# Feed-forward blocks 3, 5, 7 and 9 by eight products, block 10 by seven with a down product beside it, and all large buffers at one address remainder

## The chip, the core and the metric

The kernel runs on one core of one Trainium2 chip. The time is device microseconds (us) from launch to end. The median of 3 runs of the kernel before is 2426.34 us (2423.76 to 2428.74). The engines are named as in the profile: PE is TensorE's matmuls and PEld its weight loads, DVE is VectorE, ACT is ScalarE, POOL is GpSimd, and SP is SyncE, which here only issues DMAs.

## What is computed

Two layers over 256 rows of width 2048, float32. Layer 0 mixes with gated linear attention, layer 1 with an indexer and top-64 attention. After each mixer stands the same feed-forward step, and this is what the change touches:

```
def swiglu(h, w1, w3, w2):
    return (jax.nn.silu(h @ w1) * (h @ w3)) @ w2
...
    x = x + y
    x = x + swiglu(rmsnorm(x, norm_ffn[i]), ffn_w1[i], ffn_w3[i], ffn_w2[i])
return rmsnorm(x, norm_final)
```

`w1` and `w3` are 2048 x 5632, `w2` is 5632 x 2048. Each of them is read once from HBM per layer, in pieces of 512 x 512 (1 MB).

## The kernel before

**Precision.** TensorE multiplies in fp32r. Each operand is split in two: a high part (a cast) and a low part (what the cast left over). A product is then three matmuls: high by high, high by low, low by high. For a piece of weights ACT writes the high part `wh` (L135) and DVE the low part `wl` (L136); both come from `split_w`. The buffers `raw` (4), `wh` (3) and `wl` (3) are rings in the pool `wp`. Loads into `raw` stand in SP's queue in the order of use, so SP waits for the oldest of the four to be split.

**Feed-forward, up.** The 5632 columns are walked in 11 blocks of 512 (`b` from 0 to 10). For one block, h is seen as four parts: rows 0-127 and 128-255 by columns 0-1023 and 1024-2047. Sums and differences of these parts, the *forms* `A11`, `F7`, `A12`, `N22`, `F5`, `F3`, `F6`, lie ready in a pool called `fz` (tiles `fh...`, `fl...`). One product of a form with 1024 x 512 weights is 8 x 3 = 24 matmuls of 512 columns. There are two ways through a block:

- `plain` takes four products for each of w1 and w3, eight in all: 192 matmuls, 8 pieces loaded and split, no sums of weights.
- `pair` takes w1 and w3 together and needs seven products: 168 matmuls. It splits 14 pieces, since three of the seven products have sums of weights for an operand. These sums are made in place. DVE adds two (`plus`, L405), and DMAs that add in memory, issued by POOL, make two more (`plus_dma`, L408, two pieces each). The pieces that are summed live in four fixed homes: `v0`, `v1`, `v2` in `fz` and `g3` in the pool `res`. `turn` swaps which two hold `va` (summed by DMA) and which `vb` (summed by DVE). The products of a `pair` stand in the order A11, F5, F3, F6, F7, A12, N22; F6 waits for the first two adding DMAs, N22 for the other two.

**Feed-forward, down.** The block's result, tiles `u`, is transposed and split by `split_t` (in steps that `tick()` puts between the matmuls that follow) into a tile `g0`, `g1` or `g2`. `pieces` multiplies two such blocks with their 1024 rows of w2: 4 x 2 steps of 24 matmuls, with the sums added into `x`. A deque `down` holds these steps; `ffn` puts one step at each `yield` of `pair` or `plain`. A `pair` has eight yields, so it takes all eight steps. What is not done this way is returned by `ffn` and done afterwards by `residual`, which also starts the norm of the next stage or, at the end of the program, the final norm (`gemm_tail` for the last 512 columns).

**Which block goes which way (before).** `pair` is taken while `down` is not empty. A deque whose generator has given its last step but has not yet been asked again still counts as not empty. So blocks 0, 1 and 10 are plain, and blocks 2 to 9 are pairs. Blocks 2, 4, 6, 8 carry eight down steps each; blocks 3, 5, 7, 9 carry none. Blocks 8, 9 and 10 are left for `residual`: 4 x 3 x 24 = 288 matmuls per layer.

**Order on an engine.** Each engine works through its own list, in order; the lists come from a scheduler that places the instructions as they are written, with some moved ahead. A `pair`'s four home loads stand in SP's list among the `raw` loads.

**Addresses.** Pools follow each other in every partition of SBUF: `cst`, `res` (x, g), `wp` (raw, wh, wl), `cm` (u), `sm` (small), and then the pool of the stage (`gp`, `fz`, `dp`, at the end `fp`). In the built program, x, g, raw, wh, wl and u start at addresses with remainder 192 by 256. The stage's pool starts at remainder 128, and so do its tiles: the forms `fh`/`fl`, `v0` to `v2`, the operands `hh`/`hl` of the mixers' projections, and in `gemm_tail` the first `wh`/`wl` (taken from `fp`). In the pool `dp` some smaller tiles have other remainders.

Of the kernel before, what the change touches and what calls it, by code (L numbers as in the profile page):

```python
# [12 lines left out]
F32 = mybir.dt.float32  # L13
# [6 lines left out]
P = 128  # L20
# [3 lines left out]
NB = 512  # L24
# [31 lines left out]
def trunk(  # L56
# [9 lines left out]
    cst = ctx.enter_context(tc.tile_pool(name="cst", bufs=1))  # L66
# [3 lines left out]
    sm = ctx.enter_context(tc.tile_pool(name="sm", bufs=2))  # L70
# [13 lines left out]
            nc.sync.dma_start(x[t][n], x2[t, :, n * NB:(n + 1) * NB])  # L84


    neghalf = cst.tile([P, 8], F32, name="neghalf")
    nc.gpsimd.memset(neghalf, -0.5)
    warm = sm.tile([P, 8], F32, tag="warm", bufs=1, name="warm")
# [4 lines left out]
    cols = cst.tile([P, 72], F32, name="cols")  # L94


    sm.tile([P, 8], F32, tag="pad", bufs=1, name="pad")

    def gains(c0, srcs):

# [14 lines left out]
    def tick():  # L115

        while side:
            try:
                return next(side[0])
            except StopIteration:  # L120
                side.popleft()
# [9 lines left out]
    def split_w(raw, pool=wp):  # L131

        wh = pool.tile([P, 4, NB], F32R, tag="wh", bufs=3 if pool is wp else 1, name="wh")
        wl = pool.tile([P, 4, NB], F32R, tag="wl", bufs=3 if pool is wp else 1, name="wl")
        nc.scalar.copy(wh, raw)  # L135
        nc.vector.tensor_sub(wl, raw, wh.bitcast(F32))  # L136
        return wh, wl
# [70 lines left out]
    def split_t(src, hi, lo):  # L208

        for kk in range(2):  # L210
            tr = tr_p.tile([P, 2, SEQ], F32, tag="tr", name="tr")
            for t in range(NT):
                for k in range(2):
                    c = (2 * kk + k) * P
                    nc.tensor.transpose(tr[:, k, t * P:(t + 1) * P], src[t][:, c:c + P], ident)
            sl = slice(2 * kk, 2 * kk + 2)
            nc.scalar.copy(hi[:, sl, :], tr)
            nc.vector.tensor_sub(lo[:, sl, :], tr, hi[:, sl, :].bitcast(F32))
            yield
# [122 lines left out]
    def scaled(r, f, tag, w=NT):  # L342
        o = sm.tile([P, w], F32, tag=tag, name=tag)
        nc.gpsimd.tensor_scalar_mul(o, r, f)
        return o
# [13 lines left out]
    def hi_lo(i):  # L359
        g = res.tile([P, 2, 4, SEQ], F32R, tag=f"g{i}", name=f"g{i}")  # L360
        return g[:, 0], g[:, 1]

    def flush():
        while side:
            tick()
# [83 lines left out]
    def plain(nrm, ws, c0, done):  # L449

        for q, w in zip("12", ws):
            acc = [acc_p.tile([P, NB], F32, tag="acc", name="acc") for _ in range(3)]
            for g in range(4):
                raw = wp.tile([P, 4, NB], F32, tag="raw", bufs=RAW, name="raw")
                nc.sync.dma_start(raw, w[g * NB:(g + 1) * NB, c0:c0 + NB].rearrange("(k p) n -> p k n", p=P))
                wh, wl = split_w(raw)
                for bank, form, start, stop in ((0, "A11", True, True), (1, "F7", True, True)) if g < 2 else \
                        ((0, "A12", False, True), (2, "N22", True, True)):
                    hi, lo = nrm.forms[form]
                    for j in range(4):  # L460
                        k = 4 * (g % 2) + j
                        for i, (l_, r_) in enumerate(((hi, wh), (hi, wl), (lo, wh))):
                            nc.tensor.matmul(acc[bank], l_[:, k, :], r_[:, j, :], start=start and k == i == 0,  # L463
                                             stop=stop and k == 7 and i == 2, skip_group_check=not start)
                        if j % 2:
                            tick()
                if g == 1:
                    s1 = nrm.pool.tile([P, NB], F32, tag="s1", bufs=1, name="s1")
                    nc.scalar.copy(s1, acc[0])
                    nc.vector.tensor_add(s1, s1, acc[1])  # L470
                    yield
            nc.vector.tensor_sub(s1, s1, acc[2])
            done("1" + q, acc[0])
            done("2" + q, s1)
# [24 lines left out]
    def ffn(layer, nrm):  # L499

        w1, w3, w2 = ffn_w1[layer], ffn_w3[layer], ffn_w2[layer]
        sc = {}
        parts = []
        down = deque()
        for b in range(DFF // NB):
            us = [None] * NT

            def done(q, v):
                t = int(q[0]) - 1
                if q[1] == "1":  # L510
                    us[t] = cm.tile([P, NB], F32, tag="u", name="u")
                    nc.scalar.activation(us[t], v, AF.Tanh, scale=sc["h"][:, t:t + 1])
                    nc.vector.scalar_tensor_tensor(us[t], us[t], 1.0, v, op0=ALU.add, op1=ALU.mult)
                else:
                    nc.vector.scalar_tensor_tensor(us[t], us[t], sc["r2"][:, t:t + 1], v, op0=ALU.mult, op1=ALU.mult)

            for slot, _ in enumerate(pair(nrm, w1, w3, b * NB, b // 2 % 2, done) if down else plain(nrm, (w1, w3), b * NB, done)):
                if b == 0 and slot == 0:
                    flush()
                    r = nrm.rstd()  # L520
                    sc["h"] = scaled(r, 0.5, "rh")
                    sc["r2"] = sm.tile([P, NT], F32, tag="r2", name="r2")
                    nc.gpsimd.tensor_tensor(sc["r2"], r, sc["h"], op=ALU.mult)
                while down:
                    try:
                        next(down[0])
                        break
                    except StopIteration:
                        down.popleft()
            hi, lo = hi_lo(b % 3)  # L530
            side.append(split_t(us, hi, lo))
            parts.append((hi, lo, b * NB))
            if b % 2 and b < 8:
                down.append(pieces(w2, parts))
                parts = []
        while down:
            for _ in down.popleft():
                pass
        return w2, parts
# [480 lines left out]
    with tc.tile_pool(name="gp", bufs=2) as gp:  # L1020
        n0.begin(gp)
        down = gla(n0, gp)
        flush()
    with tc.tile_pool(name="fz0", bufs=1) as fz:
        n1.begin(fz)
        residual(gla_w_out[0], down, n1.update)
        down = ffn(0, n1)
        flush()
    with tc.tile_pool(name="dp", bufs=2) as dp:
# [3 lines left out]
        down = dsa(n2, dp)  # L1033
        flush()
    with tc.tile_pool(name="fz1", bufs=1) as fz:
        n3.begin(fz)
        residual(dsa_w_out[0], down, n3.update)
        down = ffn(1, n3)
        flush()
# [56 lines left out]
```

## Time and profile before

| | |
|---|---|
| median of 3 runs | 2426.34 us |
| profiled execution | 2430.86 us |
| its span, first to last instruction | 2429.1 us |
| mean granted TensorE clock | 0.973 |
| PE busy | 2281.5 us (94%) |
| DVE busy | 1645.9 us (68%) |
| ACT busy | 1183.5 us (49%) |
| HBM read | 489.59 MB |

The profile is of one execution. Matmuls are pipelined, so that one lasts about 390 ns while the next begins some 227 ns after it; the busy time of PE is the union. Where a stage is dense, the distance from one matmul's start to the next is the number to read. A window table gives, for a stretch of the span, its length, the busy time of each engine with the number of its instructions (x), the granted TensorE clock, and the share and rate of the DMA engines.

### The profile page before, as it was taken

How to read it: one execution, taken by the hardware profiler on the slowest of the kernel's cores; microseconds unless marked ns; L12 is line 12 of the kernel's file. 1: busy time of each engine (PE TensorE's matmuls, PEld its weight loads, DVE VectorE, ACT ScalarE, POOL GpSimd, SP SyncE). 2: the span in 40 equal slices, each digit the busy share in tenths (PEclk: the TensorE clock that was granted, in tenths of full speed). 3: DMA queues.
4: the chain of work that ended last, by engine and by line, in shares of the span. 5: the costliest groups of instructions: out<-in, count | busy, mean ns of one | idle time of the engine just before them, and what ended most of it. 6: DMA issues, size and time to landing. Idle time of an engine off the chain costs nothing.

```text
span 2429.1 us, 25156 instructions
## 1 busy us (share of the span) xinstructions
PE 2281.5 (94%) x10199; PEld 1857.5 (76%) x10199; DVE 1645.9 (68%) x1348; ACT 1183.5 (49%) x1053; POOL 112.8 (5%) x159
## 2 busy tenths in 40 slices
PE   9999999998897979989999999999988979889798
PEld 7888888876675867768888888888876867768687
DVE  6555456677886878865556655565786778878754
ACT  5545455454454445544444454454444545545443
POOL 0000000000000000000100000000000000000000
PEclk9999999999999989999999999999998999989899
DMA  8555466586877968775554545566677977779663
GB/s 280 164 174 180 148 219 232 172 233 194 232 242 207 286 184 222 229 205 187 182 173 139 191 157 174 174 219 212 176 235 201 293 182 225 230 190 311 138 218 112
DMA packets 254773, 493.36 MB, mean 203 GB/s; under 512 B 8200, under 2 KB 20832, under 8 KB 254528
## 3 DMA queue, kind: packets, MB, share of 16 engines
q1 hardware_dynamic: 219856, 423.33, 51.1%
q0 software_dynamic: 33792, 67.11, 16.0%
q8 instruction: 80, 1.31, 0.2%
q10 hardware_dynamic: 1008, 1.31, 0.2%
q14 instruction: 37, 0.30, 0.0%
HBM read 489.59 MB, written 2.12 MB: 202 GB/s over the span
## 4 chain that ended last, share of the span: by engine, by line
PE 59%; issue 21%; DMA 9%; DVE 8%; ACT 2%; POOL 1%; SPq 0%; POOLq 0%; ACTq 0%; DVEq 0%
PE acc L201 11%; PE acc L203 11%; PE acc L202 11%; PE acc L463 10%; DMA g<-in_ffn_w 6%; PE acc L393 6%; DVE wl L136 5%; DMA v<-in_ffn_w 3%; PE down L490 2%; ACT wh L135 2%; PE down L491 2%; PE down L489 2%; DVE v L405 1%; POOL v L408 1%; PE trq L827 0%
## 5 line engine op out<-in xcount | busy, mean ns | idle before, releaser
L192 DVE TENSOR_TENSOR wl<-raw,wh 128x2048 fp32r<-128x2048 f32 (+3 forms) x161 | 350.1, 2176 | 314.8 <-ACT wh L191 314.6
L136 DVE TENSOR_TENSOR wl<-raw,wh 128x2048 fp32r<-128x2048 f32 x179 | 409.5, 2289 | 184.7 <-ACT wh L135 184.7
L135 ACT CAST wh<-raw 128x2048 fp32r<-128x2048 f32 x179 | 342.3, 1912 | 392.6 <-PE down L491 144.3
L191 ACT CAST wh<-raw 128x2048 fp32r<-128x2048 f32 (+3 forms) x161 | 291.9, 1815 | 278.8 <-PE acc L203 217.7
L136 DVE TENSOR_TENSOR wl<-v,wh 128x2048 fp32r<-128x2048 f32 x120 | 272.7, 2286 | 83.1 <-ACT wh L135 83.1
L201 PE MATMUL acc<-wh,hh 128*128 128x512 f32 (+3 forms) x832 | 327.1, 393 | 0.0
L135 ACT CAST wh<-v 128x2048 fp32r<-128x2048 f32 x120 | 227.4, 1904 | 198.9 <-DMA v<-in_ffn_w 99.9
L203 PE MATMUL acc<-wh,hl 128*128 128x512 f32 (+3 forms) x832 | 318.4, 383 | 0.0
L202 PE MATMUL acc<-wl,hh 128*128 128x512 f32 (+3 forms) x832 | 317.0, 381 | 0.5 <-DVE wl L192 0.5
L393 PE MATMUL acc<-wh,fhF 128*128 128x512 f32 x512 | 216.5, 426 | 59.3 <-ACT wh L135 59.2
L393 PE MATMUL acc<-wl,fhF 128*128 128x512 f32 x512 | 216.0, 422 | 30.9 <-DVE wl L136 30.9
L490 PE MATMUL down<-wl,g 128*128 128x512 f32 x512 | 204.0, 398 | 9.3 <-DVE wl L136 9.3
L393 PE MATMUL acc<-wh,flF 128*128 128x512 f32 x512 | 212.2, 414 | 0.0
L491 PE MATMUL down<-wh,g 128*128 128x512 f32 x512 | 202.9, 396 | 0.0
L489 PE MATMUL down<-wh,g 128*128 128x512 f32 x512 | 200.3, 394 | 0.0
L203 PEld LDWEIGHTS acc<-wh,hl 128*128 128x128 f32 x832 | 156.2, 188 | 30.8
L202 PEld LDWEIGHTS acc<-wl,hh 128*128 128x128 f32 x832 | 156.6, 188 | 30.3 <-issue 1.7
L201 PEld LDWEIGHTS acc<-wh,hh 128*128 128x128 f32 x832 | 156.5, 188 | 28.9 <-issue 1.9
L393 PEld LDWEIGHTS acc<-wh,fhF 128*128 128x128 f32 x512 | 103.9, 205 | 91.2 <-ACT wh L135 68.3
L201 PE MATMUL acc<-wh,g 128*128 128x512 f32 x424 | 167.2, 394 | 0.0
L203 PE MATMUL acc<-wh,g 128*128 128x512 f32 x424 | 165.5, 390 | 0.0
L202 PE MATMUL acc<-wl,g 128*128 128x512 f32 x424 | 165.4, 390 | 0.0
(282 smaller groups left out, 3608.6 us busy)
## 6 DMA issues: line engine op xcount, KB each, us to landing
raw<-in_ffn_w SPq DMA_DIRECT2D x200, 1024.0 KB, 5.8
v<-in_ffn_w SPq DMA_DIRECT2D x48, 1024.0 KB, 6.6
v<-in_ffn_w POOLq DMA_DIRECT2D x48, 1024.0 KB, 9.4
raw<-in_dsa_w_in SPq DMA_DIRECT2D x48, 1024.0 KB, 5.1
raw<-in_gla_w_in SPq DMA_DIRECT2D x40, 1024.0 KB, 5.1
raw<-in_gla_w_out SPq DMA_DIRECT2D x16, 1024.0 KB, 5.2
g<-in_ffn_w SPq DMA_DIRECT2D x16, 1024.0 KB, 6.7
g<-in_ffn_w POOLq DMA_DIRECT2D x16, 1024.0 KB, 13.3
```

Of the source, the lines that this page charges most:

```text
L135: nc.scalar.copy(wh, raw)
L136: nc.vector.tensor_sub(wl, raw, wh.bitcast(F32))
L191: a = nc.scalar.copy(wh[:, sl, :n], raw[:, sl, :n])
L192: v = nc.vector.tensor_sub(wl[:, sl, :n], raw[:, sl, :n], wh[:, sl, :n].bitcast(F32))
L201: nc.tensor.matmul(acc[t][:, :n], hi[:, k, ts_], wh[:, k, :n], start=start, stop=False)
L202: nc.tensor.matmul(acc[t][:, :n], hi[:, k, ts_], wl[:, k, :n], start=False, stop=False)
L203: nc.tensor.matmul(acc[t][:, :n], lo[:, k, ts_], wh[:, k, :n], start=False, stop=last)
L393: nc.tensor.matmul(acc, l_[:, k, :], r_[:, j, :], start=start and k == i == 0, stop=stop and k == 7 and i == 2, skip_group_check=not start)
L463: nc.tensor.matmul(acc[bank], l_[:, k, :], r_[:, j, :], start=start and k == i == 0, stop=stop and k == 7 and i == 2, skip_group_check=not ...
L489: nc.tensor.matmul(acc[t], hi[:, k, ts_], wh[:, k, :], start=start, stop=False)
L490: nc.tensor.matmul(acc[t], hi[:, k, ts_], wl[:, k, :], start=False, stop=False)
L491: nc.tensor.matmul(acc[t], lo[:, k, ts_], wh[:, k, :], start=False, stop=last)
```

## The change

Three things. (1) The way through a block is now chosen by its number: blocks 2, 4, 6, 8 and 10 are pairs, the others plain. (2) The down steps of blocks 8 and 9 are put in the deque too, so block 10 carries them; `residual` is left with block 10 alone, 96 matmuls. (3) A tile of 64 bytes is put ahead in `cst`, and a dummy in `sm` grows from 32 to 96 bytes. In the built program x, g, raw, wh, wl, u, and the stage's forms, homes and `hh`/`hl` then all start at remainder 0 by 256.

```
+    cst.tile([P, 16], F32, name="pad")
     neghalf = cst.tile([P, 8], F32, name="neghalf")
...
-    sm.tile([P, 8], F32, tag="pad", bufs=1, name="pad")
+    sm.tile([P, 24], F32, tag="pad", bufs=1, name="pad")
...
-            for slot, _ in enumerate(pair(nrm, w1, w3, b * NB, b // 2 % 2, done) if down else plain(nrm, (w1, w3), b * NB, done)):
+            for slot, _ in enumerate(pair(nrm, w1, w3, b * NB, b // 2 % 2, done) if b in range(2, 11, 2) else plain(nrm, (w1, w3), b * NB, done)):
...
-            if b % 2 and b < 8:
+            if b % 2:
                 down.append(pieces(w2, parts))
                 parts = []
```

Per layer this is four pairs fewer, one pair more, and the same w2 work in other places. Lines of the changed kernel are one higher than those of the one before.

First place: SP's list in layer 0, from the last loads of block 2 on. Before, block 3 is a pair. `v_4058`, `v_4060` are its homes v0, v1, and `v_4054`, `g_4056` its v2, g3; L380 with `raw` is a piece of weights that is multiplied once, L482 a piece of w2.

```order
L482 DMA raw<-in_ffn_w 128x4x512
L380 DMA v_4058<-in_ffn_w 128x4x512
L380 DMA v_4060<-in_ffn_w 128x4x512
L482 DMA raw<-in_ffn_w 128x4x512 x2
L380 DMA raw<-in_ffn_w 128x4x512 x2
L380 DMA v_4054<-in_ffn_w 128x4x512
L380 DMA g_4056<-in_ffn_w 128x4x512
L380 DMA raw<-in_ffn_w 128x4x512 x2
L482 DMA raw<-in_ffn_w 128x4x512 x2
```

Now block 3 is plain (its pieces are L456), and the home loads between are those of block 4: `v_4332`, `v_4334` are v0, v1, and `v_4336`, `g_4338` are v2, g3.

```order
L483 DMA raw<-in_ffn_w 128x4x512
L381 DMA v_4332<-in_ffn_w 128x4x512
L381 DMA v_4334<-in_ffn_w 128x4x512
L483 DMA raw<-in_ffn_w 128x4x512 x2
L456 DMA raw<-in_ffn_w 128x4x512 x2
L381 DMA v_4336<-in_ffn_w 128x4x512
L381 DMA g_4338<-in_ffn_w 128x4x512
L456 DMA raw<-in_ffn_w 128x4x512 x6
L483 DMA raw<-in_ffn_w 128x4x512 x2
```

The home loads stand at the same places of the list, but what they load is used a whole block later.

Second place: DVE's list in layer 0, inside block 3. Before, a stretch of the pair of block 3; each `wl` is one split of 2.29 us in the trace, L405 a sum of two pieces, and y, w, s sums of products.

```order
L136 TENSOR_TENSOR wl<-raw,wh 128x2048
L405 TENSOR_TENSOR v_4060<-v_4060,raw 128x2048
L423 TENSOR_TENSOR y<-acc,s_4111 128x512
L136 TENSOR_TENSOR wl<-raw,wh 128x2048
L136 TENSOR_TENSOR wl<-v_4054,wh 128x2048
L136 TENSOR_TENSOR wl<-g_4056,wh 128x2048
L136 TENSOR_TENSOR wl<-v_4058,wh 128x2048
L136 TENSOR_TENSOR wl<-v_4060,wh 128x2048
L431 TENSOR_TENSOR w<-acc,s_4111 128x512
```

Now, the middle of the plain block 3, up to the first split of block 4 (`v_4332`):

```order
L219 TENSOR_TENSOR g_4054<-tr,g_4054 128x512 x2
L137 TENSOR_TENSOR wl<-raw,wh 128x2048
L471 TENSOR_TENSOR s_4132<-s_4132,acc 128x512
L137 TENSOR_TENSOR wl<-raw,wh 128x2048 x2
L514 SCALAR_TENSOR_TENSOR u<-u,acc 128x512
L473 TENSOR_TENSOR s_4132<-s_4132,acc 128x512
L137 TENSOR_TENSOR wl<-raw,wh 128x2048
L514 SCALAR_TENSOR_TENSOR u<-u,s_4132 128x512
L137 TENSOR_TENSOR wl<-raw,wh 128x2048
L471 TENSOR_TENSOR s_4265<-s_4265,acc 128x512
L137 TENSOR_TENSOR wl<-v_4332,wh 128x2048
```

No split of block 3 reads a home any longer, so none of them stands behind an adding DMA.

Third place: SP's list at the end of layer 0. Before, block 10 is plain (L455), and `residual` loads twelve pieces of w2 (L185) ahead of the next mixer's weights:

```order
L380 DMA raw<-in_ffn_w 128x4x512 x2
L455 DMA raw<-in_ffn_w 128x4x512 x8
L185 DMA raw<-in_ffn_w 128x4x512 x6
L758 DMA rb<-in_rel_bias 32x16
L185 DMA raw<-in_ffn_w 128x4x512 x6
L185 DMA raw<-in_dsa_w_in 128x4x400 x4
```

Now block 10 is a pair with eight down steps (L483), and `residual` loads four pieces:

```order
L483 DMA raw<-in_ffn_w 128x4x512 x3
L381 DMA raw<-in_ffn_w 128x4x512 x2
L483 DMA raw<-in_ffn_w 128x4x512 x3
L186 DMA raw<-in_ffn_w 128x4x512 x4
L186 DMA raw<-in_dsa_w_in 128x4x400
L759 DMA rb<-in_rel_bias 32x16
L186 DMA raw<-in_dsa_w_in 128x4x400 x3
```

Eight pieces of w2 have moved from `residual` into block 10.

## The prediction

> **What bounds the kernel now.** I read a table of windows first, one window for each feed-forward block, cut at the first matmul of each block. Columns: start:end and length, then busy us (and instructions) of PE, PEld, DVE, ACT and POOL, then the granted clock, the DMA share and GB/s. Ten rows are blocks 2 to 10 and `residual` of layer 0; the seven below are layer 1: block 2, blocks 3+4, 5+6, 7+8, block 9, block 10, and `residual` to the end of the span.
>
> ```profile
> 485.92:571.08 85.16, 83.33 (x370) 68.23 (x369) 69.50 (x46) 44.62 (x27) 5.41 (x4) 1.00 0.85 247
> 571.08:630.64 59.56, 44.48 (x177) 34.10 (x176) 40.28 (x26) 28.29 (x18) 5.17 (x4) 0.91 0.77 200
> 630.64:718.20 87.56, 84.01 (x369) 68.22 (x368) 76.45 (x50) 45.53 (x28) 5.19 (x4) 1.00 0.83 248
> 718.20:777.60 59.40, 44.69 (x177) 34.15 (x176) 40.28 (x26) 28.30 (x18) 5.19 (x4) 0.91 0.77 200
> 777.60:866.09 88.49, 84.34 (x370) 68.12 (x368) 76.39 (x50) 45.33 (x28) 5.19 (x4) 1.00 0.83 246
> 866.09:926.05 59.96, 45.63 (x177) 35.28 (x176) 40.36 (x26) 28.29 (x18) 5.19 (x4) 0.89 0.77 198
> 926.05:1015.12 89.07, 85.49 (x369) 69.32 (x368) 76.74 (x50) 45.51 (x28) 5.19 (x4) 0.98 0.83 244
> 1015.12:1072.00 56.88, 44.62 (x178) 34.49 (x177) 41.56 (x27) 28.54 (x18) 5.19 (x4) 0.91 0.65 148
> 1072.00:1117.24 45.24, 45.24 (x206) 37.11 (x204) 27.29 (x21) 19.63 (x16) 0.00 (x0) 1.00 0.61 210
> 1117.24:1186.05 68.81, 68.81 (x320) 56.68 (x318) 38.47 (x35) 31.54 (x38) 0.68 (x4) 1.00 0.54 174
> 1718.60:1802.95 84.35, 83.19 (x369) 68.22 (x368) 69.48 (x46) 44.63 (x27) 5.23 (x4) 1.00 0.85 249
> 1802.95:1952.56 149.61, 133.02 (x545) 106.20 (x544) 116.93 (x75) 73.83 (x46) 10.37 (x8) 0.93 0.80 225
> 1952.56:2102.41 149.85, 132.89 (x545) 106.31 (x544) 116.91 (x75) 73.85 (x46) 10.37 (x8) 0.93 0.79 224
> 2102.41:2250.95 148.54, 132.24 (x545) 105.59 (x544) 117.11 (x75) 74.03 (x46) 10.37 (x8) 0.92 0.81 227
> 2250.95:2309.38 58.43, 45.91 (x177) 35.61 (x176) 41.52 (x27) 28.53 (x18) 5.18 (x4) 0.88 0.63 144
> 2309.38:2354.60 45.22, 45.22 (x205) 37.11 (x204) 27.46 (x21) 19.62 (x16) 0.00 (x0) 1.00 0.61 210
> 2354.60:2429.08 74.48, 66.24 (x295) 54.30 (x293) 37.35 (x36) 28.20 (x32) 1.11 (x2) 0.98 0.41 141
> ```
>
> Three kinds of block are to be seen. A pair with down steps (blocks 2, 4, 6, 8) is nearly all PE: 83 to 85 us busy. Block 10, plain, is all PE: 45.24 of 45.24. A pair alone (3, 5, 7, 9), a *quiet* pair, has the fewest matmuls and still takes 56.9 to 60 us, of which PE is busy for some 45: 12 to 15 us are holes, at a clock of 0.88 to 0.91 instead of 1.00. So eight products take less time there than seven. What holds the seven is in POOL's timeline of block 3 (start, length, what, and in brackets the idle time before and who ended it):
>
> ```profile
> 580.42 1.28 POOL L408 DMA_DIRECT2D v<-in_ffn_w  x1 [49.62 <-issue]
> 590.18 1.30 POOL L408 DMA_DIRECT2D g<-in_ffn_w  x1 [8.47 <-DMA v<-in_ffn_w]
> 601.07 1.29 POOL L408 DMA_DIRECT2D v<-in_ffn_w  x1 [9.60 <-DMA g<-in_ffn_w]
> 609.99 1.30 POOL L408 DMA_DIRECT2D g<-in_ffn_w  x1 [7.63 <-DVE wl L136]
> ```
>
> The four adding DMAs start about 10 us apart, and twice one waits for the one before to land. The first two lie between the splits of F5 and of F6, the last two between those of F6 and of N22. Four in a row need about 40 us. In 85 us of a pair with down steps that is covered; among the 168 matmuls of a quiet pair it is not.
>
> **The way of the blocks.** Durations come from the profiled execution of 2430.86 us (span 2429.1); the sum is made against that and carried over to the median of 2426.34, which is 4.5 lower.
>
> *Quiet pairs become plain.* Layer 0: 59.56 + 59.40 + 59.96 + 56.88 = 235.80 us now. A plain block is 45.24 (row of block 10, which also follows a pair and already pays the transposes of the block ahead of it), so four are 180.96: **-54.84**. The 24 matmuls more that each takes are in the 45.24. The splits fall from 14 to 8 a block, and neither POOL nor a home is waited for. Late next would be DVE at 27.29 or the DMA share of 0.61: neither is near.
>
> *Pairs 4, 6, 8 follow a plain block.* They take 87.56 + 88.49 + 89.07 = 265.12 us now. Block 2 is the one pair that already follows a plain block: 85.16. The rest of the work is the same, but after a quiet pair the homes are loaded late, since N22 of that pair still reads them; in the new list the loads stand a block ahead, as they did for block 2. 3 x 85.16 = 255.48: **-9.64**. I keep the hold of 1.8 us (85.16 less 83.33 busy) that remains in block 2, where F6 waits for the second adding DMA.
>
> *Block 10 and `residual`.* Now 45.24 + 68.81 = 114.05. Then block 10 is a pair with down steps, 85.16, and `residual` loses 192 of its 288 matmuls at 0.2268 us (worked out below), 43.55, so it is 25.26. What covered is gone in one place: the first product of `residual` was that of block 8, long ready, and is now block 10's own, which has to be transposed, cast and split first. The 48 down matmuls at the end of block 10 cover the making of `u`, not the split. No row shows this wait. From below it is 0 (in the row of `residual` PE has no idle time: 68.81 of 68.81), from above the 1.8 us of block 2's hold; I take 1. Together 111.42: **-2.63**. Eight norm steps now go with 96 matmuls instead of 288. That is still ahead of DVE: of its 38.47 us, eight splits of 2.29 go, which leaves 20 beside PE's 25.
>
> Layer 0 in all: -67.11.
>
> *Layer 1.* Blocks 3 to 8: 149.61 + 149.85 + 148.54 = 448.00, then 3 x (45.22 + 84.35) = 388.71: **-59.29**. Block 9: 58.43 to 45.22, **-13.21**. Block 10 with the end: 45.22 + 74.48 = 119.70, then 84.35 + 74.48 - 43.55 + 1.5 = 116.78, **-2.92**. The 1.5 are 0.5 for the split and 1 for the tail: the closing work of rows 0-127 (sum, norm, scaling, DVE and ACT in order) was hidden behind 36 matmuls and now has 12, 2.7 us, and what stands behind it on DVE and ACT is the closing work of rows 128-255, which ends the kernel. The bounds are 0 and 5.5 (the tail of 74.48 - 66.24 = 8.2, less the 2.7); I stay near 0, since only the DVE and ACT steps queue and not the chain. Layer 1 in all: -75.42.
>
> Sum of (1) and (2): **-142.5 us**.
>
> **The remainders.** Next the starts of matmuls in dense stretches (start, length, engine, line, what). First the last gemm: the first 12 matmuls of each half have `wh`, `wl` in `fp` (remainder 128) against `g` (192); from the 19th to the 25th both are at 192.
>
> ```profile
> 2404.16 0.39 PE L152 MATMUL acc<-wh,g 128*128 128x512 f32 x1
> ...
> 2406.96 0.39 PE L152 MATMUL acc<-wh,g 128*128 128x512 f32 x1
> ...
> 2408.34 0.39 PE L152 MATMUL acc<-wh,g 128*128 128x512 f32 x1
> ...
> 2409.70 0.39 PE L152 MATMUL acc<-wh,g 128*128 128x512 f32 x1
> ```
>
> 12 matmuls in 2.80 us are 233.3 ns each; 6 in 1.36 us are 226.7. Line, shapes and `g` are the same; the home of `wh`, `wl` is not. Next 24 matmuls of a pair, `wh` at 192 and the form at 128, and behind them 24 down matmuls, both at 192:
>
> ```profile
> 532.84 0.39 PE L393 MATMUL acc<-wh,fhF 128*128 128x512 f32 x1
> ...
> 538.33 0.39 PE L489 MATMUL down<-wh,g 128*128 128x512 f32 x1
> ...
> 543.77 0.39 PE L393 MATMUL acc<-wh,fhA 128*128 128x512 f32 x1
> ```
>
> 5.49 / 24 = 228.8 ns, and 5.44 / 24 = 226.8 (0.2268 above). So unequal remainders cost 2 to 6.6 ns a matmul. After the change they are equal, at 0. The matmuls that gain: forms, 6 x 192 + 5 x 168 = 1992 a layer, 3984 in all; and those on `hh`/`hl`, 3 x 736 by the rows of the groups, of which this is one:
>
> ```profile
> L203 PE MATMUL acc<-wh,hl 128*128 128x512 f32 x736 | 289.4, 393 | 0.0
> ```
>
> 3984 + 2208 = 6192 at 2.1 ns (between the 2.0 above and somewhat more, as I count no others): **-13.0 us**. All of it is on the path, as PE bounds every stage that is left. Equal remainders at 0 are not in the trace, only at 192. The bounds: no gain (0), or, if 0 is as bad as the worst row, 6192 x (233.3 - 228.8) and some 2900 matmuls on `g` x (233.3 - 226.8): +47 us. I take the row with equal remainders, the nearest. DVE and ACT I cost at nothing: a split of `v` (128 into 192) takes what one of `raw` (192 into 192) takes, 2286 and 2289 ns by these groups:
>
> ```profile
> L136 DVE TENSOR_TENSOR wl<-raw,wh 128x2048 fp32r<-128x2048 f32 x179 | 409.5, 2289 | 184.7 <-ACT wh L135 184.7
> ...
> L136 DVE TENSOR_TENSOR wl<-v,wh 128x2048 fp32r<-128x2048 f32 x120 | 272.7, 2286 | 83.1 <-ACT wh L135 83.1
> ```
>
> [...] The rows above differ by 6.6 ns with nothing changed but a buffer's place, so I follow the rows.
>
> **Sum.** 142.5 + 13.0 = 155.5 us less: 2430.86 becomes 2275.3, and from the median, 2426.34 - 155.5 = 2270.8. Forecast **2271 us**.
>
> **Rivals.**
> - *The remainders do nothing* (the change does not do what its third part says). For it: the rows with equal remainders are at other lines or parts of a gemm than most of those that should gain. Against: the last gemm. Time: 2271 + 13 = 2284. Chance 0.12.
> - *Pairs 4 to 8 keep their hold.* If the 2.4 to 3.9 us over block 2 come not from the homes but from the adding DMAs meeting more loads, they stay. 9.64 come back in layer 0, and in layer 1 between that and 19.7 (448.00 less three quiet pairs at 58.43 and three pairs at 84.35); I take 12: 2293. Against it: DMA share and rate in block 2 are as high (0.85, 247) as in the later ones. Chance 0.10.
> - *Late pieces after a pair* (the slower end). SP is in order, and in the first place of the list the home loads v2, g3 stand ahead of six pieces of the plain block and wait for N22's split. If SP were held there until four pieces, the whole ring, were used up, PE would lose four groups of 24 matmuls, 21.8 us, at the four joints of pair to plain in each layer: 2271 + 174 = 2445. It decides from 19.4 us a joint. Against it: N22 is split ahead of its matmuls, 72 or more matmuls (N22 and the down steps) follow that need only pieces loaded already, and DMA has room. A loss of a few us at a joint is likelier. Chance 0.02 for the full loss, 0.06 for one of 1 to 3 us a joint (2279 to 2295).
> - *Remainder 0 is worse than 192*: up to 2284 + 47 = 2331. Chance 0.03.
> - *More is won*: the hold of F6 goes too, 1.8 and 1.2 us in ten pairs: 2256. Chance 0.05.
>
> The forecast itself, 2261 to 2281, has the remaining 0.62. Range **2256 to 2293**: it takes in the remainders at nothing and the pairs that keep their hold, and leaves out the late pieces, the bad remainder and a little on each side. A measurement here can tell about 0.2%, 5 us. Faster by more than that: 0.97, as every case but the full loss lies below 2421; within: 0.01; slower: 0.02.
>
> **What would show it.** In windows cut in the same way: plain blocks 3 to 9 at 44 to 46 us with PE busy throughout and the clock at 1.00; pairs 4 to 10 at 84 to 86; `residual` of layer 0 at 24 to 28; 40 adding DMAs instead of 64 and still about 10 us apart. Dense matmuls on forms and `hh` 227 ns apart instead of 229: if they stay at 229, the third part has no effect. A plain block with holes at its start would show the late pieces; a pair of 88 us the hold that stays. The forecast is wrong if PE is idle for more than some 30 us in the feed-forward stages, or if the rest of the kernel, which the change leaves alone but for addresses, moves by more than its part of the 13 us.

## The result, and the profile after

| | us | ratio to before, 95% interval |
|---|---|---|
| kernel before, 4 runs on the same chip | 2427.06 (2423.76 to 2428.74) | |
| changed kernel, 4 runs | **2293.0** (2285.74 to 2298.71) | 0.9448 [0.9418, 0.9477] |
| forecast | 2271, range 2256 to 2293 | |

The change takes off 134 us where the forecast had 155: the sign and the bulk are right, and 22 us are missing, at the very end of the range. The profiled execution took 2298.71 us (span 2296.9), the longest of the four; against it the sum of the prediction, 2275.3, is **23.4 short**. The HBM read falls from 489.59 to 464.43 MB: `w1` and `w3` are not read just once, since the adding DMAs of a pair read four of its pieces a second time, and 24 such pieces of 1 MB are saved.

First the table of windows of the changed kernel, cut at the first matmul of each block as before: blocks 2, 3, 4, 6, 8, 10 and `residual` of layer 0, then of layer 1 blocks 2, 3, 4, 6, 8, block 10 with the wait behind it, and the end. (Blocks 5, 7, 9 read like block 3.) Columns: start:end and length, busy us (and instructions) of PE, PEld, DVE, ACT and POOL, granted clock, DMA share, GB/s.

```profile
483.98:568.63 84.65, 82.97 (x370) 68.11 (x368) 67.32 (x45) 44.70 (x27) 5.42 (x4) 1.00 0.87 261
568.63:613.09 44.46, 44.46 (x202) 36.83 (x200) 27.77 (x20) 18.86 (x14) 0.00 (x0) 1.00 0.52 165
613.09:697.69 84.60, 82.94 (x370) 68.11 (x368) 67.29 (x45) 44.69 (x27) 5.17 (x4) 1.00 0.88 261
...
742.15:829.24 87.09, 84.83 (x369) 69.26 (x368) 67.57 (x45) 44.69 (x27) 5.19 (x4) 0.98 0.87 253
...
873.70:957.79 84.09, 82.95 (x369) 68.13 (x368) 67.30 (x45) 44.70 (x27) 5.19 (x4) 1.00 0.88 263
...
1002.25:1089.31 87.06, 84.64 (x369) 69.12 (x368) 67.48 (x45) 44.68 (x27) 5.87 (x8) 0.98 0.75 205
1089.31:1117.50 28.19, 26.26 (x130) 21.21 (x129) 19.50 (x26) 16.08 (x29) 0.00 (x0) 1.00 0.47 150
1647.66:1734.16 86.50, 84.68 (x369) 69.25 (x368) 67.59 (x45) 44.67 (x27) 5.23 (x4) 0.98 0.87 255
1734.16:1778.62 44.46, 44.46 (x201) 36.82 (x200) 27.76 (x20) 18.86 (x14) 0.00 (x0) 1.00 0.50 165
1778.62:1866.05 87.43, 84.87 (x370) 69.26 (x368) 67.56 (x45) 44.68 (x27) 5.18 (x4) 0.98 0.86 253
...
1910.51:1999.11 88.60, 86.09 (x369) 70.17 (x368) 67.64 (x45) 44.67 (x27) 5.19 (x4) 0.96 0.86 249
...
2043.57:2130.09 86.52, 84.70 (x370) 69.25 (x368) 67.59 (x45) 44.70 (x27) 5.19 (x4) 0.98 0.88 255
...
2174.55:2264.51 89.96, 85.91 (x378) 70.00 (x376) 70.66 (x48) 48.93 (x31) 5.19 (x4) 0.98 0.71 199
2264.51:2296.90 32.39, 22.39 (x96) 17.86 (x96) 15.64 (x25) 8.90 (x21) 1.11 (x2) 0.90 0.17 66
```

The plain blocks are what was forecast, and better: 44.46 us, all of it PE. What is off is the pairs. Three of layer 0 lie at 84.1 to 84.7; the other two and all of layer 1 at 86.5 and more, with 1.8 to 2.6 us without a matmul (4.05 in the last, whose window takes in the wait behind it) and a clock of 0.96 to 0.98. Something inside a pair takes 2 to 4 us more than I had kept for it.

Where it is, the groups of PE show at once (line, shapes, count | busy us, mean ns | idle before them and who ended it). These are the form F's matmuls in pairs:

```profile
L394 PE MATMUL acc<-wl,fhF 128*128 128x512 f32 x320 | 130.2, 407 | 17.3 <-DVE wl L137 17.3
...
L394 PE MATMUL acc<-wh,fhF 128*128 128x512 f32 x320 | 128.9, 403 | 3.1 <-ACT wh L136 3.1
```

Together 20.4 us of idle PE stand in front of a split. The forms F5, F3, F6 and F7 share this row. PE's timeline of block 6, layer 0, says which it is: the second half of F6 (start, length, what, idle before it):

```profile
775.84 0.39 PE L394 MATMUL acc<-wh,fhF 128*128 128x512 f32 x1
...
779.16 0.50 PE L394 MATMUL acc<-wh,fhF 128*128 128x512 f32 x1 [0.44 <-ACT wh L136]
781.49 0.50 PE L394 MATMUL acc<-wl,fhF 128*128 128x512 f32 x1 [1.82 <-DVE wl L137]
...
782.95 0.63 PE L394 MATMUL acc<-wh,flF 128*128 128x512 f32 x1
783.38 0.63 PE L394 MATMUL acc<-wh,fhF 128*128 128x512 f32 x1
...
785.71 0.40 PE L490 MATMUL down<-wh,g 128*128 128x512 f32 x1
```

F6 should take 24 x 0.2268 = 5.44 us and takes 785.71 - 775.84 = 9.87. There are two losses in it. PE waits 0.44 us for the high part and 1.82 for the low part of the second piece. Then its matmuls come 0.43 us apart instead of 0.227 (782.95, 783.38): the granted clock is 0.50 from 781.99 to 785.40, for 3.4 us, which costs another 1.7. What the split waited for stands in ACT's and POOL's timelines of the same block:

```profile
777.20 1.91 ACT L136 CAST wh<-g 128x2048 fp32r<-128x2048 f32 x1 [7.41 <-DMA g<-in_ffn_w]
```

```profile
752.92 1.29 POOL L409 DMA_DIRECT2D v<-in_ffn_w  x1 [95.08 <-issue]
762.04 1.30 POOL L409 DMA_DIRECT2D g<-in_ffn_w  x1 [7.82 <-DVE y L424]
777.42 1.29 POOL L409 DMA_DIRECT2D v<-in_ffn_w  x1 [14.08 <-DMA g<-in_ffn_w]
```

ACT stood idle for 7.41 us until the second adding DMA had landed. That DMA was issued at 762.04 and landed at 777.1, 35.0 us after the block's first matmul at 742.15; then the cast takes 1.91 and the low part 2.29 before PE can go on. Measured from the first matmul of F6 to that of the down step behind it, in all ten pairs, F6 takes 7.44, 7.40, 9.87, 6.88, 9.85 us in layer 0 and 9.28, 9.60, 10.75, 9.28, 9.41 in layer 1: 89.8 instead of 54.4, so **35.4 us** are lost there. 20.4 of them are the idle time of the two rows above. About 11 are half clock: eight stretches of 3.41 us, less the holes in them, lose half of their length, 13 us, of which 1.9 fall on the down steps behind F6. The rest comes with the longer matmuls at the edges of the holes (some 0.3 us in each F6 that saw no half clock).

### The profile page after: what moved, and what is told of

It is laid out like the page before. It is cut to its first block, busy times and chain, and to the rows that moved or that the text cites. A ratio compares the mean times of both kernels' runs of the same rounds, so it can differ in the third digit from the quotient of the medians.

```text
span 2296.9 us, 25246 instructions
## 1 busy us (share of the span) xinstructions
PE 2256.8 (98%) x10343; PEld 1862.9 (81%) x10343; DVE 1526.7 (66%) x1298; ACT 1122.6 (49%) x1023; POOL 81.6 (4%) x135
## 3 DMA queue, kind: packets, MB, share of 16 engines
q0 software_dynamic: 21120, 41.95, 10.6%
HBM read 464.43 MB, written 2.12 MB: 203 GB/s over the span
## 4 chain that ended last, share of the span: by engine, by line
PE 57%; issue 30%; DMA 7%; DVE 3%; ACT 2%; POOL 1%; SPq 0%; POOLq 0%; ACTq 0%
PE acc L204 11%; PE acc L202 10%; PE acc L203 10%; PE acc L464 10%; PE acc L394 5%; DMA g<-in_ffn_w 4%; DMA v<-in_ffn_w 2%; PE down L490 2%; PE down L491 2%; PE down L492 2%; DVE wl L137 2%; ACT wh L136 1%; POOL v L409 1%; DVE wl L193 0%; PE tr L216 0%
## 5 line engine op out<-in xcount | busy, mean ns | idle before, releaser
L137 DVE TENSOR_TENSOR wl<-raw,wh 128x2048 fp32r<-128x2048 f32 x217 | 496.8, 2290 | 242.9 <-ACT wh L136 241.8
L492 PE MATMUL down<-wh,g 128*128 128x512 f32 x640 | 249.6, 390 | 0.0
L490 PE MATMUL down<-wh,g 128*128 128x512 f32 x640 | 248.3, 391 | 0.0
L137 DVE TENSOR_TENSOR wl<-v,wh 128x2048 fp32r<-128x2048 f32 x72 | 164.4, 2287 | 51.4 <-ACT wh L136 51.4
L136 ACT CAST wh<-v 128x2048 fp32r<-128x2048 f32 x72 | 137.6, 1911 | 107.2 <-PE acc L394 44.7
L464 PE MATMUL acc<-wh,fhA 128*128 128x512 f32 x384 | 150.7, 393 | 0.2
L464 PE MATMUL acc<-wh,flA 128*128 128x512 f32 x384 | 149.6, 390 | 0.0
L464 PE MATMUL acc<-wl,fhA 128*128 128x512 f32 x384 | 149.6, 390 | 0.0
L394 PE MATMUL acc<-wl,fhF 128*128 128x512 f32 x320 | 130.2, 407 | 17.3 <-DVE wl L137 17.3
L491 PEld LDWEIGHTS down<-wl,g 128*128 128x128 f32 x640 | 120.6, 188 | 26.3
L490 PEld LDWEIGHTS down<-wh,g 128*128 128x128 f32 x640 | 121.0, 189 | 25.3
L492 PEld LDWEIGHTS down<-wh,g 128*128 128x128 f32 x640 | 120.6, 188 | 24.9
```

The costliest lines, as they stand in the source:

```text
L394: nc.tensor.matmul(acc, l_[:, k, :], r_[:, j, :], start=start and k == i == 0, stop=stop and k == 7 and i == 2, skip_group_check=not start)
L490: nc.tensor.matmul(acc[t], hi[:, k, ts_], wh[:, k, :], start=start, stop=False)
L491: nc.tensor.matmul(acc[t], hi[:, k, ts_], wl[:, k, :], start=False, stop=False)
L492: nc.tensor.matmul(acc[t], lo[:, k, ts_], wh[:, k, :], start=False, stop=last)
```

## The experiments

Lines named are those of the changed kernel. Each kernel was run beside the kernel before, which gave 2427.7, 2429.1 and 2426.8 us on the three chips.

**The two halves of the change apart.** `e1_order_alone` is the changed kernel at the old addresses, `e2_places_alone` the old order at the new ones:

```
 e1 (against the changed kernel)                    e2 (against the kernel before)
-    cst.tile([P, 16], F32, name="pad")             +    cst.tile([P, 16], F32, name="pad")
...
-    sm.tile([P, 24], F32, tag="pad", ...)          -    sm.tile([P, 8], F32, tag="pad", ...)
+    sm.tile([P, 8], F32, tag="pad", ...)           +    sm.tile([P, 24], F32, tag="pad", ...)
```

> The new choice of blocks and the moved down steps, with all buffers at their old addresses (remainders 192 and 128). Theory 'unequal remainders cost time': dense matmuls on forms and hh at about 229 ns instead of 227, and some 6192 x 2 = 12 us slower than the changed kernel, about 2305 us (ratio to before 0.950). Rival 'remainders do nothing': the same as the changed kernel, 2293 us (0.945), and the same spacing.

> The kernel before with the two pads alone (all remainders 0), blocks as before. Theory 'unequal remainders cost time': spacing 227 ns, and 2208 matmuls on hh, 1152 of plain blocks and 1344 of pairs with down steps gain 2 ns each, 9 us, while the quiet pairs, which wait for the adding DMAs, gain nothing: about 2418 us (0.996). Rival 'remainders do nothing': 2427 us (1.000).

Measured: e1 2280.27 us (2276.6 to 2284.55), ratio 0.9394 [0.9379, 0.9409]; e2 2427.45, ratio 1.0004 [0.9993, 1.0016]. Neither theory had e1 right: without the third part of the change the time is not 12 us longer, nor the same, but 13 shorter than the first result. It is close to what the prediction had for the first two parts alone, 2426.3 - 142.5 = 2284. e2 has the time of its rival. The rows of windows are the pair of block 6, layer 0, in e1; the stretch of blocks 2 to 9 of layer 0 and of layer 1 in e2; and the same two stretches in the kernel before:

```profile
742.74:827.08 84.34, 83.21 (x369) 68.23 (x368) 67.21 (x45) 44.61 (x27) 5.19 (x4) 1.00 0.87 262
```

```profile
484.04:1070.10 586.06, 517.16 (x2176) 414.11 (x2176) 461.08 (x294) 294.81 (x183) 41.70 (x32) 0.96 0.79 222
1714.13:2301.57 587.44, 519.35 (x2177) 416.21 (x2176) 461.13 (x294) 294.52 (x183) 41.52 (x32) 0.95 0.79 222
```

```profile
485.92:1072.00 586.08, 516.59 (x2178) 411.91 (x2177) 461.56 (x294) 294.41 (x183) 41.71 (x32) 0.96 0.80 222
1718.60:2309.38 590.78, 527.24 (x2177) 421.94 (x2176) 461.95 (x294) 294.86 (x183) 41.53 (x32) 0.93 0.79 221
```

In e1 the pair of block 6 takes 84.34 us at full clock, against 88.49 before the change and 87.09 after it. Its F6 products take 5.62 to 6.91 us, and only 7.4 us are lost there in all ten (against 24 x 0.2288 = 5.49 us each); no half clock is seen but at the very end. In e2 the matmuls on forms come 227 ns apart instead of 229, and yet the medians differ by 0.3 us where 9 were forecast. Its eight pairs of layer 0 take what they took before (586.2 us from the first matmul of block 2, which stands 0.18 us ahead of the row's start, against 586.08); those of layer 1 take 3.3 us less. These are single executions of kernels whose runs spread over 9 to 11 us, and in the profiles the stretches outside the pairs are 5.5 us shorter in e2. So by the medians the pairs give back what the rest gains; where, one profile of each cannot show.

**The wait itself.** `e3_slot_before_f6` is the changed kernel with one of the eight down steps moved ahead of F6. The last `yield` of `pair`, behind N22, goes to before F6; the products and DMAs stay as they are, and PE has 5.44 us more work before it needs the adding DMA. `e4_filler` keeps the order and fills the hole instead, with ten matmuls between the halves of F6 into a tile that nothing reads:

```
 e3                                                  e4 (in product(), before the matmuls of a half)
     product(b2, vc, "F3", False, True)             +    if form == "F6":
     yield                                          +        if c == 1:
+    yield                                          +            fill = tr_p.tile([P, NB], F32, ...)
     b3 = bank()                                    +            for _ in range(10):
     product(b3, va, "F6", ...)                     +                nc.tensor.matmul(fill, hi[:, 0, :],
...                                                 +                    first_wh[:, 0, :], ...)
     done("22", y)                                  +        first_wh = wh
-    yield
```

> The changed kernel with one yield of pair moved from its end to ahead of F6, so that two down steps (48 matmuls) and not one lie between F3 and F6. Theory 'what was missed is F6's wait for the second adding DMA, made longer by the half clock that follows it': F6 takes 5.44 us in all ten pairs instead of 6.9 to 10.8 (89.8 us in all in the profile), no stretch at half clock is left but the one at the end, and some 35 us go, less 0 to 10 us at the ends of pairs, where one down step and not two now covers the making of u: 2258 to 2268 us (0.931 to 0.935). Rival 'the four adding DMAs in a row bound the pair': the hold moves to N22 and the time stays at 2293 us (0.945).

> The changed kernel with ten matmuls of 512 columns, whose result nobody reads, between the two halves of F6 (100 in all, 22.7 us of work). They keep PE busy during the wait and leave the wait itself as it is. Theory 'part of what was missed is the clock': no half clock in the pairs, F6 takes 7.7 to 8.2 us everywhere, 1.7 us less in each of the seven pairs that had a half-clock stretch in the profile and 0.3 to 1.3 more in the other three: about 10 us faster, 2283 us (0.941). Rival 'the wait is all, the clock is nothing': F6 as before or up to 2.3 us longer, 2293 to 2316 us (0.945 to 0.954).

Measured: e3 **2260.48** (2260.41 to 2260.53), ratio 0.9312 [0.9298, 0.9326]; e4 2284.57 (2284.02 to 2285.62), 0.9412 [0.9398, 0.9426]. The windows of e3 for the pairs of block 6 of both layers, and its POOL timeline of the first:

```profile
738.00:820.64 82.64, 82.64 (x369) 68.19 (x368) 66.89 (x44) 44.93 (x27) 5.19 (x4) 1.00 0.88 264
1887.50:1970.15 82.65, 82.65 (x370) 68.18 (x368) 66.90 (x44) 44.92 (x27) 5.19 (x4) 1.00 0.88 264
```

```profile
748.77 1.29 POOL L409 DMA_DIRECT2D v<-in_ffn_w  x1 [91.45 <-issue]
757.45 1.30 POOL L409 DMA_DIRECT2D g<-in_ffn_w  x1 [7.38 <-DMA v<-in_ffn_w]
771.47 1.29 POOL L409 DMA_DIRECT2D v<-in_ffn_w  x1 [12.72 <-DMA g<-in_ffn_w]
```

The adding DMAs are no faster to speak of: the second lands at about 771.2, 33.2 us after the first matmul of the block. But F6's second half now needs its piece 5.44 us later, and every one of the ten F6 takes 5.44 us. Pairs are all PE, 82.64 of 82.64, as is everything from block 2 to block 10 of either layer (591.06 of 591.06 and 591.10 of 591.10 us). That is the whole of the loss and more. In e4 each F6 takes 7.71 us, 34 x 0.2268, so the hole is exactly filled; the half clock is gone everywhere but at the end, although the second adding DMA still lands 33.5 us after the block's first matmul. So the half clock follows from the hole, though e4 alone is a weak proof of it: with landings like these the changed kernel shows only two half-clock stretches (below), and the rows at the end of this document say more. (The time of e4 shows no gain: the changed kernel itself was not run on that chip, and on another it took 2279.84 us.)

**The changed kernel again.** The first result and the batches above come from different chips, so the changed kernel was run unaltered once more, as `r1_changed_again` (r1):

> The changed kernel itself, unaltered, beside the next three on the same chip. If its time belongs to the kernel: about 2293 us (0.945) again, F6 at 7 to 10 us in most pairs and several half-clock stretches. If the first result was one chip's slow DMA: nearer the 2280 us that the new order had at the old places.

Measured: 2279.84 us (2277.53 to 2281.6), ratio 0.938 [0.9366, 0.9394], 13 less than the first time, while the kernel before was 2.1 slower than there. Again F6 carries the difference: 6.41 to 9.48 us each, 20.2 lost instead of 35.4, and the half clock came twice instead of in seven pairs. Its row of the group shown above has 13.6 instead of 17.3:

```profile
L394 PE MATMUL acc<-wl,fhF 128*128 128x512 f32 x320 | 126.7, 396 | 13.6 <-DVE wl L137 13.6
```

So the changed kernel as it stands has no one time: by these two profiles it depends on how late an adding DMA lands, which differs from chip to chip. The mean landing of the second one after the block's first matmul is 34.6 us in the first profile, 33.8 here, and 32.9 in e1 at the old addresses. By an estimate F6 runs without a wait when it is there by about 32.4: in the profile of the changed kernel F6 begins 33.7 us after the block's first matmul, the first matmul that needs the low part of its second piece comes 13 matmuls or 2.9 us later, and the cast and the low part take 1.9 and 2.3 before that. (In e1 the F6 whose piece landed at 32.34 has no idle time, and one at 32.59 has 0.09 us.) Against the same number in e1, 2280.27, the 12 us of the remainders do not show at all: outside F6 the profile of r1 is 9.6 us shorter, and at F6 it loses 20.2 us where e1 loses 7.4. That is not because PE comes to F6 earlier with its faster matmuls: F6 begins 33.70 us after the block's first matmul in r1 and 33.74 in e1. What moved is the landing, by 0.9 us.

**The remainders, with the wait covered.** Three kernels with e3's order, on one chip: `e5_slot_old_places` with the old addresses, `e6_slot_equal_192` with all large buffers at 192 by 256 instead of 0, and `e7_slot_128_apart` with the stage's pool at 64 and the rings `wh`, `wl` and g at 192, 128 bytes apart:

```
 e5                                      e6                                 e7
-    cst.tile([P, 16], ..., name="pad")  -    cst.tile([P, 16], ...)        -    cst.tile([P, 16], ...)
-    sm.tile([P, 24], ...)                                                  -    sm.tile([P, 24], ...)
+    sm.tile([P, 8], ...)                                                   +    sm.tile([P, 56], ...)
```

> The kernel with the yield moved ahead of F6 (2260.5 us at remainder 0), with all buffers at their old addresses (192 and 128). Here PE waits for no adding DMA, so the worth of the remainders is seen bare. Theory 'unequal remainders cost 2 ns a matmul': 6192 matmuls, about 12 us slower, 2272 us (0.936). Rival 'their worth is small or of the other sign': 2255 to 2263 us.

> The same order, all large buffers at remainder 192 by 256 (the pad in cst left out, the one in sm kept). Theory 'equality counts, not the value 0': spacing 227 ns and 2260 us as with 0. Rival '0 itself counts': spacing 229 ns, 2272 us.

> The same order, raw, wh, wl, g at remainder 192 and the stage's pool at 64 by 256, so 128 apart. If what counts is the remainder by 128: 227 ns, 2260 us. If it is the remainder by 256 or more: 229 ns or worse, 2272 us or more.

| | forms and `hh`/`hl` against `wh`/`wl` | us | ratio, 95% interval |
|---|---|---|---|
| e3 | 0 and 0 | 2260.48 | 0.9312 [0.9298, 0.9326] |
| e6 | 192 and 192 | 2260.69 | 0.9303 [0.9289, 0.9317] |
| e5 | 128 and 192 | 2272.04 | 0.9349 [0.9335, 0.9363] |
| e7 | 64 and 192 | 2291.79 | 0.9430 [0.9414, 0.9445] |

One plain block shows it, block 3 of layer 0 in e5, e6 and e7, each one row of windows:

```profile
568.97:613.84 44.87, 44.87 (x202) 36.85 (x200) 28.52 (x21) 18.83 (x14) 0.00 (x0) 1.00 0.49 170
```

```profile
566.38:610.85 44.47, 44.47 (x202) 36.83 (x201) 28.43 (x21) 18.87 (x14) 0.00 (x0) 1.00 0.51 172
```

```profile
574.46:619.95 45.49, 45.49 (x201) 36.95 (x200) 28.62 (x21) 18.82 (x14) 0.00 (x0) 1.00 0.50 167
```

All three are PE from end to end, at full clock, with the same matmuls, and take 44.87, 44.47 and 45.49. Of the four cases tried the two with equal remainders by 256 have one time, at 0 and at 192; and it is not the remainder by 128 that counts, by which e7 would be as good as e6. Other distances were not tried. 11.4 us lie between e5 and e6, 31.1 between e7 and e6. This is the -13.0 of the prediction, to 2 us, once nothing waits in its place.

**Block 10.** `e8_two_steps_kept` keeps e3's last two down steps of block 10 for after its products; `e9_block10_plain` is e3 with block 10 of each layer plain:

```
 e8, in ffn()
-                while down:
+                while down and not (b == 10 and slot > 5):
 e9, in ffn()
-  ... pair(nrm, w1, w3, b * NB, b // 2 % 2, done) if b in range(2, 11, 2) else plain(...)
+  ... pair(nrm, w1, w3, b * NB, b // 2 % 2, done) if b in range(2, 10, 2) else plain(...)
```

> e3 with the last two steps of the way down held back in block 10 of each layer, so that they run after its last product, with the split of the block's own operand inside them. Theory (the waits of e3 at the start of the residual, 0.39 + 1.03 + 0.30 = 1.7 us a layer, are a matter of what stands beside the split): they go, 2260.5 - 2 x 1.7 = 2257, and nothing else appears. Rival (the two steps only move; the products A12 and N22 without a step between them then wait for the casts of their own operand, 1 us or more at each, or the adding DMAs, so that the time stays at 2260 or rises).

> e3 with block 10 of each layer written plain, eight products, its operand still taken by the residual and the steps of the way down of blocks 8 and 9 drained after it. Theory (a pair at block 10 is worth its 24 matmuls of 226.7 ns, 5.4 us a layer, less the 1.7 us that the residual's first product waits, which the drained steps would hide here): 2260.5 + 2 x (5.4 - 1.7) = 2268. Rival (a pair's drained steps and sums cost as much as the product it saves): 2260 or less.

Measured: e8 **2256.61** (2256.03 to 2256.81), ratio 0.9296 [0.9276, 0.9316]; e9 2268.94 (2268.82 to 2269.96), 0.9348 [0.9329, 0.9368]. Both as the theory had them. What e8 removes is the wait at the start of `residual`. In the changed kernel ACT's timeline there reads

```profile
1089.51 1.90 ACT L192 CAST wh<-raw 128x2048 fp32r<-128x2048 f32 x1 [3.49 <-DVE x L497]
1091.32 1.07 ACT L218 CAST g<-tr 128x512 fp32r<-128x512 f32 x2
```

The cast of block 10's own operand (`g<-tr`) stands behind a cast of 1.90 us for the next weights, and PE waits 1.60 us for it and 0.33 for the low part. In e8 it lies beside the two kept steps; the windows of its block 10 with these steps, and of the stretch of `residual` behind it, have no idle PE:

```profile
992.87:1076.49 83.62, 83.62 (x377) 68.87 (x376) 68.91 (x47) 45.90 (x29) 5.87 (x8) 1.00 0.76 214
1076.49:1105.00 28.51, 28.51 (x144) 24.06 (x143) 21.41 (x28) 17.65 (x31) 3.32 (x13) 1.00 0.48 159
```

e8 is the best of these: 170 us under the kernel before, 36 under the first result of the change. From e9 to e8, on one chip, the pair at block 10 with its wait covered is worth 12.3 us in two layers; from e9 to e3, on another, 8.5.

## Why the prediction was right, and where it was wrong

*Quiet pairs become plain*: right. 45.24 was forecast for each of the plain blocks 3 to 9, less 0.4 by the remainders, and 44.46 came (44.86 in e1), PE throughout and the clock at 1.00. The rival of late pieces fell: no plain block has a hole at its start, in either layer.

*Pairs 4, 6, 8 follow a plain block and become like block 2*: right in what becomes of them. At the old addresses (e1) block 6 takes 84.34 and no longer 88.49. That the late loads of the homes were the reason was not tested by itself. The rival that gave 2293, pairs that keep their old hold, hit the time by luck and not by its mechanism: the hold that came is not the 2.4 to 3.9 us over block 2, for block 2 itself has it, 86.50 in layer 1 where it was 84.35.

*"I keep the hold of 1.8 us (85.16 less 83.33 busy) that remains in block 2, where F6 waits for the second adding DMA"*: **this is the step that failed**, by its size. The hold was kept as a constant. In block 2 of the kernel before, F6 reads

```profile
519.64 0.39 PE L393 MATMUL acc<-wh,fhF 128*128 128x512 f32 x1
...
524.73 0.51 PE L393 MATMUL acc<-wl,fhF 128*128 128x512 f32 x1 [1.82 <-DVE wl L136]
...
527.38 0.39 PE L489 MATMUL down<-wh,g 128*128 128x512 f32 x1
```

that is 7.74 us, 2.25 more than 24 x 0.2288 = 5.49; in layer 1 it is 1.45 more. With the windows of block 2 the sum so holds 5 x 2.25 and 5 x 1.45, 18.5 us at ten F6, of which 15 (5 x 1.8 and 5 x 1.2) are idle time and none is half clock. Measured were 35.4 in the profiled execution, 20.2 in the profile of the second chip and 7.4 in e1. In the profiled execution 16.9 of the 23.4 missing stand at F6 and 1.9 more in the half clock that runs on behind it: the idle time came to 20.4, and the half clock, 13 us, had no term at all. A wait at the edge of its cover is not a cost of its own; it is the difference of two moments. PE came to F6 at the same moment, 33.7 us after the block's first matmul, with either pace of the matmuls. The adding DMA landed 0.9 (r1) to 1.7 us (first profile) later than in e1. And the holes grew: in block 2 of the kernel before, the stretch of 3.41 us with F6's hole has PE busy for 1.83 us (521.07 to 524.48) and in layer 1 for 2.25 (1753.27 to 1756.68), and the clock behind it is 1.00; in the first profile of the changed kernel seven such stretches have 1.15 to 1.62, and the clock behind them is 0.50, which adds 1.7 us a time. On the second chip, where the loss happened to come near the 18.5, the time was 2279.84, within the 2261 to 2281 of the forecast itself.

The signs that the prediction gave say the same: 40 adding DMAs came, but not 10 us apart. In block 6 they start at 752.92, 762.04 and 777.42, as the second takes 15.1 us. The prediction took the 10 us from a quiet pair, where the second takes 10.6 us; in block 2 of the kernel before it takes 14.6.

*The remainders*: the size was right (-13.0; 11.4 between e5 and e6), and the sentence *"All of it is on the path, as PE bounds every stage that is left"* was right but for one point in each pair. Outside F6 r1 is 9.6 us shorter than e1; at F6, 12.8 more are lost, since the adding DMA lands later. In the kernel's time the gain is seen only where a down step covers F6. No gain at all (the prediction's bound of 0, and its rival at 2284) would make e5, e6 and e7 one time; they are 2272, 2261 and 2292, so the measurement decides against it for these tiles.

*Block 10 and `residual`*: the direction was right (e9). The wait of `residual`'s first product, taken at 1 us in layer 0 and 0.5 in layer 1 since no row showed it, measured 1.93 and 2.15: 2.6 us more. With the 18.8 at F6 and behind it that makes 21.4 of the 23.4. The tail after the last matmul grew from 8.2 to 9.5 us, near the 1 that was taken. The remaining 2 us are differences of both signs, in many stages, and were not followed.

*More is won* (the hold of F6 goes too, 2256, given 0.05) did not come by itself, but it is what e3 and e8 made of it: 2260.5 and 2256.6.

What stays open is why the second adding DMA lands 34.6, 33.8 or 32.9 us after the block's first matmul. It waits for the first one, which takes 8.4 to 9.0 us on the average of a profile, and then takes 13.5 to 14.5 itself while loads of pieces run beside it. At the old places it came earlier on both chips (32.9 in e1 against 33.8 in e3, 33.0 in e5 against 33.8 in r1). It goes with the pace of the matmuls: in the seven profiles of the new order with equal remainders it comes at 33.5 to 34.6 on the average, and in the three with unequal ones at 32.7 to 33.0, earliest in e7, which has the slowest matmuls of all. The place alone fits less well, since e6, at other places than r1 but with the same pace (and e3's order), has 33.5 on the same chip. The same kernel on two chips differs by 0.8 as well. No run changed the pace alone, so the cause is not shown.

## What to carry to other kernels

A wait that remains "at 1 or 2 us" is a margin that has run out, and not a term to be carried over: ask when the transfer lands and when its user comes, and what moves either. Here a landing that was 0.9 us later, ten times, took back the 10 us that faster matmuls had won elsewhere. Moving one piece of independent work ahead of the user (one `yield`, 5.44 us, here) was worth more than that gain: e3 lies 32 us under the first time of the changed kernel and 19 under the second. A change of half a per cent was measured bare only after that wait was covered.

## What the runs showed of the hardware

**In these profiles half clock came on one grid of 3.4133 us, behind a stretch that was about half empty.** All half-clock stretches of the profile of the changed kernel begin at multiples of 3.4133 us from each other (to some 12 ns, over 1.5 ms), and last 3.413 or twice that, the end aside. Laid on that grid, rows of windows come in twos, the stretch with F6's hole and the one behind it: block 2 and block 4 of layer 0, then block 6, then block 2 of layer 1.

```profile
519.17:522.58 3.41, 1.73 (x9) 1.11 (x8) 2.47 (x2) 3.41 (x3) 0.44 (x1) 1.00 0.85 202
522.58:525.99 3.41, 3.41 (x15) 2.80 (x16) 3.41 (x2) 1.78 (x2) 0.00 (x0) 1.00 1.14 209
648.87:652.28 3.41, 1.75 (x8) 1.16 (x7) 3.08 (x2) 3.41 (x3) 0.00 (x0) 1.00 0.90 144
652.28:655.69 3.41, 3.41 (x16) 2.80 (x16) 3.41 (x2) 1.81 (x2) 0.00 (x0) 1.00 1.11 212
778.58:781.99 3.41, 1.15 (x4) 0.64 (x4) 2.85 (x2) 3.41 (x3) 0.13 (x1) 1.00 0.81 124
781.99:785.40 3.41, 3.41 (x10) 2.66 (x9) 3.41 (x2) 0.72 (x1) 0.00 (x0) 0.50 1.13 202
1683.06:1686.47 3.41, 1.59 (x8) 0.88 (x6) 2.42 (x2) 3.41 (x3) 0.54 (x1) 1.00 0.69 123
1686.47:1689.88 3.41, 3.41 (x9) 2.64 (x10) 3.41 (x2) 1.14 (x1) 0.00 (x0) 0.51 1.13 208
```

A stretch with PE busy for 1.73 or 1.75 us of 3.41 is followed by full clock, one with 1.59 or 1.15 (47% and 34% of it) by half. In the two profiles of the changed kernel every stretch entered at full clock with 1.62 or less was followed by half, and none with 1.73 or more, the first 11 us aside, for which the first of them records no clock. (In the kernel before and in e2, with many more such stretches, the same holds but for three: about 1.63 and 1.59 kept full clock, and 1.91 was followed by half. The ends of matmuls are modelled in a profile, so where between these numbers it turns is not shown.) By these rows an estimate is that a hole of 1.6 us in one window costs 1.6, and one of 1.8 costs 1.8 and 1.7 more (half of 3.41).

**The place of an operand changed the pace of these matmuls**: 227 ns a matmul on forms where stationary and moving operand start at the same remainder by 256 (24 of them in 5.44 us in e6), 229 where their remainders are 64 bytes apart (e5) and 232 where they are 128 apart (e7). The last two are that of e6 and what the plain block above takes more, 0.40 and 1.02 us over 192 matmuls. Why was not tried.
